# The low part of the attention scores: from two 64-row products to two 128-row products with zeros

## The chip, the cores and the metric

The kernel runs on one core of one Trainium2 chip. The metric is device time in microseconds (us), from the first to the last instruction of the program with what little lies around it; lower is better. The profile names the engines PE (TensorE, matrix products), PEld (the loads of its stationary operand), DVE (VectorE), ACT (ScalarE), POOL (GpSimd) and SP (which issues the transfers here).

## What is computed

A trunk of two layers over 1024 tokens of width 1024, in float32: differential attention with a gated MLP, then gated linear attention with a gated MLP, each behind an RMS norm. The change lies in the attention of the first layer. Cut to what matters:

```python
q_blocks = ...                                   # blocks of 128 query tokens
s = jnp.einsum('bqhmd,bkhmd->bhmqk', qb, k)      # 8 heads h, 2 maps m, 64 values d
p = jax.nn.softmax(jnp.where(mask, s, -jnp.inf), axis=-1)
a = p[:, :, 0] - lam * p[:, :, 1]
o = jnp.einsum('bhqk,bkhe->bqhe', a, v)
...
o = rms_norm(o, subln_gain) * (1.0 - lambda_init)
```

Each head has two maps of 64 values, each with a softmax of its own; the difference of the two weighs the values, and the head's output is normed over its 128 values.

## The kernel before, in words

**Precision.** PE multiplies operands of the type fp32r, which hold fewer bits than float32. So the kernel splits a float32 operand into a high part (a cast) and a low part (the rest), and adds three products: high by high, high by low, low by high. In the helper `mm3` these are lines L142 to L144.

**The scores.** For the scores two products take the place of three. For each map m a tile `QH[m]` of 128 rows holds the high part of the queries twice, in rows 0 to 63 and again in 64 to 127; `KS[m]` holds the high part of the keys beside their low part in the same manner (map 1 with the halves exchanged). One product over 128 rows (L766) therefore gives high by high and high by low. The third, low queries by high keys, is the second score product (L771). The low parts of both maps lie in one tile `QL`: map 0 in rows 0 to 63, map 1 in rows 64 to 127. So L771 contracts over 64 rows alone, map 0 over the upper half of PE's array and map 1 over the lower half.

**The loop.** `attention` runs over 8 heads, and in each over 8 query tiles i of 128 tokens. For tile i, w = (i + 1) * 128 keys count. For w up to 512 both maps share one PSUM tile of 1024 columns; for more, each map has its own, cut into two pieces (256 and 384 columns for i = 4; 512 and 256, 384 or 512 for i = 5 to 7). There are two such PSUM tiles. Behind the scores comes a chain: DVE takes mask and maximum out of PSUM (L776), ACT exponentiates (L779), POOL scales the second map (L783), DVE subtracts (L785). One tile later `transposes` turns the result on PE (`pta`, L802), ACT and DVE split it (`ah` L805, `al` L806), and every second tile `values` multiplies it with the values into `oT`.

**What fills PE meanwhile.** Between the score tiles of head h stand the units of head h + 1: the products for its queries, keys and values (`psq`, `psv`, 24 products of 512 columns for each unit), a transpose of its values (`psw`, L707), the rotary step and the stacking into `QH` and `KS`, in which POOL makes `QL` (L685; DVE does for head 0). In head 7 the first units of the output projection (`pacc`, `res` L325) stand there. Behind the last head comes the rest of that projection, and behind it the first MLP.

**The head's norm.** After every fourth tile `finish` squares `oT` on ACT (L829), keeps a scaled copy `on` (L831) in the buffer place 27, and splits the squares on DVE into `hl` (L284, L285, place 26). Later `rstd_rows` adds them over the rows on PE (`ssp`, L293 and L294), takes the reciprocal root with ACT's logarithm and exponential and some steps of DVE (L295 to L300, all in place 13), multiplies with `on` (L837) and writes the result to memory.

**What sets the order.** Each engine runs its instructions in one fixed order. That order is worked out when the kernel is built, by a planner that runs the program against its own table of costs; the kernel's text only gives the order in which work is offered to it. The buffers ("places", `slot(i)`) hold 128 rows of 1024 values each, and a new tile in a place waits for the readers of the one before it.

## Time and profile before

| | |
|---|---|
| median of three runs | 2517.71 us (2516.28 to 2519.01) |
| profiled execution: its time, its span | 2519.34 us, 2517.6 us |
| PE busy in the span | 2450.1 us (97%) |
| DVE, POOL, ACT busy | 65%, 47%, 41% |
| attention of layer 0, first score product to last transposes | about 64 to 536 us |
| one head of the middle (1 to 6) | 59.90 us |

In the timeline each row is an instruction or a run of equal ones: when the first starts, how long the row lasts, its engine, line and operation, the tile written and the tiles read, the shape, the count, and in brackets the idle time of the engine before it with what ended it. `128*128` or `64*128` ahead of a shape is the rows by columns of the stationary operand. PE's products are pipelined: a product's own length is longer than its distance to the next one, so that what a product costs PE is read from the start of one row to the start of another, not from its length or from the busy share.

### The profile page before, as it was taken

What the parts mean: (1) busy time and instruction counts of PE and PEld (TensorE: products, weight loads), DVE (VectorE), ACT (ScalarE), POOL (GpSimd) and SP (SyncE); (2) the same over time, 40 slices, a digit from 0 to 9 for tenths busy, and PEclk for the clock granted to TensorE, in tenths of its full rate; (3) what the DMA queues carried; (4) which work ended last, traced back from release to release, by engine and by line L of the source; (5) the groups of instructions that cost most, each with busy time, mean ns of one, the idle gap of its engine ahead of it and who ended that gap; (6) DMA issues with size and microseconds to landing.
All of it is one profiled execution on the core that took longest, in us unless ns stands there. A gap on an engine that the chain in (4) does not pass through costs nothing. (4 is left out here: it accounts for less than half of the span.)

```text
span 2517.6 us, 30784 instructions
## 1 busy us (share of the span) xinstructions
PE 2450.1 (97%) x11752; PEld 1995.8 (79%) x11752; DVE 1625.7 (65%) x2210; ACT 1040.6 (41%) x1630; POOL 1189.4 (47%) x723
## 2 busy tenths in 40 slices
PE   7999999998999999999999999999899999999998
PEld 6777777776788888878888998987678888887887
DVE  5577777877666666654565486487676666655455
ACT  4454544544454554432124443442345445443211
POOL 4444444425655555554423344343465555545441
PEclk9999999999999999999999999999999999999999
DMA  5222222433222222343321111124322222244331
GB/s 188 56 67 59 59 59 59 126 122 126 75 76 84 76 85 83 137 157 109 101 87 60 34 43 59 35 92 156 112 76 76 84 77 88 79 147 148 107 101 67
DMA packets 66020, 228.60 MB, mean 91 GB/s; under 512 B 8145, under 2 KB 8785, under 8 KB 65873
## 3 DMA queue, kind: packets, MB, share of 16 engines
q1 hardware_dynamic: 65872, 226.64, 27.3%
q8 instruction: 92, 1.51, 0.3%
q14 instruction: 56, 0.45, 0.1%
HBM read 163.17 MB, written 50.86 MB: 85 GB/s over the span
## 5 line engine op out<-in xcount | busy, mean ns | idle before, releaser
L325 DVE TENSOR_TENSOR res<-pacc,res 128x512 f32<-128x512 f32 x368 | 252.9, 690 | 238.1 <-PE pacc L144 237.6
L497 POOL TENSOR_TENSOR uw<-st,uw 128x512 fp32r<-128x512 f32 x190 | 290.9, 1532 | 219.8 <-ACT uw L496 212.1
L123 POOL TENSOR_TENSOR wl<-st,wh 128x1024 fp32r<-128x1024 f32 x57 | 146.0, 2568 | 203.6 <-ACT wh L122 203.6
L144 PE MATMUL pacc<-wdh,gl 128*128 128x512 f32 x512 | 200.8, 392 | 0.0
L143 PE MATMUL pacc<-wdl,gh 128*128 128x512 f32 x512 | 200.5, 392 | 0.0
L142 PE MATMUL pacc<-wdh,gh 128*128 128x512 f32 x512 | 198.6, 392 | 1.8 <-DVE res L316 1.8
L576 DVE SCALAR_TENSOR_TENSOR b<-cu,cv,b 128x1023 f32<-128x1023 f32 x44 | 63.4, 1440 | 172.5 <-ACT b L575 172.2
L496 ACT CAST uw<-st 128x512 fp32r<-128x512 f32 x190 | 118.0, 622 | 123.8 <-PE ps_z L144 54.2
L142 PE MATMUL psq<-XH,wh 128*128 128x512 f32 x384 | 156.6, 408 | 0.1
L143 PE MATMUL psq<-XL,wh 128*128 128x512 f32 x384 | 154.1, 401 | 0.1
L144 PE MATMUL psq<-XH,wl 128*128 128x512 f32 x384 | 152.6, 399 | 0.0
L626 POOL TENSOR_TENSOR gl<-st,gh 128x1024 fp32r<-128x1024 f32 x32 | 77.8, 2430 | 151.3 <-ACT gh L625 108.4
L779 ACT ACTIVATE p<-p,nmax 128x256 f32<-128x256 f32 (+7 forms) x128 | 99.1, 777 | 85.4 <-DVE nmax L776 84.2
L497 POOL TENSOR_TENSOR wh<-st,wh 128x512 fp32r<-128x512 f32 x56 | 87.1, 1555 | 80.8 <-ACT wh L496 80.8
L625 ACT CAST gh<-st 128x1024 fp32r<-128x1024 f32 x32 | 33.6, 1050 | 202.7 <-PE pacc L143 144.1
L497 POOL TENSOR_TENSOR wl<-st,wl 128x512 fp32r<-128x512 f32 x56 | 85.3, 1524 | 63.0 <-ACT wl L496 63.0
L142 PEld LDWEIGHTS pacc<-wdh,gh 128*128 128x128 f32 x512 | 96.1, 188 | 23.4 <-DVE res L316 2.6
L143 PEld LDWEIGHTS pacc<-wdl,gh 128*128 128x128 f32 x512 | 96.1, 188 | 21.7
L144 PEld LDWEIGHTS pacc<-wdh,gl 128*128 128x128 f32 x512 | 96.1, 188 | 20.9
L776 DVE CUSTOM_DVE_ANT_0 p<-s_ps,mask 128x256 f32<-128x256 f32 (+7 forms) x128 | 91.4, 750 | 30.7 <-PE pta L802 22.4
L142 PE MATMUL pacc<-wh,gh 128*128 128x512 f32 x256 | 103.2, 409 | 4.0 <-DVE res L325 4.0
L143 PE MATMUL pacc<-wl,gh 128*128 128x512 f32 x256 | 102.8, 403 | 1.5 <-POOL wl L123 1.5
(363 smaller groups left out, 7358.9 us busy)
## 6 DMA issues: line engine op xcount, KB each, us to landing
st<-in_wup_dram SPq DMA_DIRECT2D x88, 512.0 KB, 3.5
g_scr<-a SPq DMA_DIRECT2D x44, 512.0 KB, 2.6
st<-in_wdn_dram SPq DMA_DIRECT2D x44, 512.0 KB, 3.6
st<-g_scr SPq DMA_DIRECT2D x44, 512.0 KB, 3.3
r_scr<-res SPq DMA_DIRECT2D x24, 512.0 KB, 4.7
res<-r_scr SPq DMA_DIRECT2D x24, 512.0 KB, 5.7
st<-in_wqk_dram SPq DMA_DIRECT2D x16, 512.0 KB, 3.5
st<-o_scr SPq DMA_DIRECT2D x13, 512.0 KB, 3.3
```

Source lines behind the costliest of these rows:

```text
L123: (eng_lo or nc.gpsimd).tensor_tensor(lo, st, f32(hi), op=ALU.subtract)
L142: nc.tensor.matmul(ps, lhsT=ah, rhs=bh, start=first, stop=False, **kw)
L143: nc.tensor.matmul(ps, lhsT=ah, rhs=bl, start=False, stop=False, **kw)
L144: nc.tensor.matmul(ps, lhsT=al, rhs=bh, start=False, stop=last, **kw)
L325: nc.vector.tensor_tensor(res[t][:, half(dh)], ps, res[t][:, half(dh)], op=ALU.add)
L496: nc.scalar.copy(w[:, half(0)], src)
L497: nc.gpsimd.tensor_tensor(w[:, half(1)], src, f32(w[:, half(0)]), op=ALU.subtract)
L576: nc.vector.scalar_tensor_tensor(u[:, 1:], c[:, :T - 1], cv[:, n, 1:2], u[:, 1:], op0=ALU.mult, op1=ALU.add)
L625: nc.scalar.copy(hi, st)
L626: nc.gpsimd.tensor_tensor(lo, st, f32(hi), op=ALU.subtract)
L776: nc.vector.tensor_tensor_reduce(out=pm[:, :w], in0=s_ps[:, :w], in1=st["mask"][:, T - w:], scale=-0.125, scalar=3.0e38, op0=ALU.add, op1= ...
L779: nc.scalar.activation(pm[:, :w], pm[:, :w], AF.Exp, bias=nmax, scale=-1.0, accum_out=sums[:, m:m + 1])
```

## The change

The second score product contracts over 128 rows as the first does. A new tile `Z` (place 27, which `on` had) has for each map and for two query tiles at a time 128 rows by 256 columns of stationary operand. It is zeroed once by eight instructions on DVE; `low(h, g)` then copies, on ACT, the low parts of map 0 into its rows 0 to 63 and those of map 1 into its rows 64 to 127, each map into its own part, so that the rows of the other map stay zero. One such call serves the query tiles 2g and 2g + 1; `Z` holds two groups, and the copies for a group are offered two query tiles ahead of it: 64 copies of 64x256 in all. The product with all 128 rows of `KS[m]` then adds the same as the one over 64 rows did. For each map its two products now stand behind each other.

Since place 27 is taken, the norm of the head makes do with fewer places: `on` moves into the free half of the squares' tile, and the reciprocal root `y` goes into the place of `hl` (26 or 19), which is free by then; it is taken there only after the sums are read. The norm of the second layer passes its old place and is as before.

```diff
-            QH, QL, KS, _, _ = st[h]
+            QH, _, KS, _, _ = st[h]
...
+            if i % 2 == 0 and (i + 2 < NT or h + 1 < HEADS):
+                low(h + (i + 2) // NT, (i + 2) % NT // 2)
...
             for m in range(2):
-                for c, n in parts:
-                    nc.tensor.matmul(s[m][:, c:c + n], lhsT=QH[m][:, qt], rhs=KS[m][:, c:c + n],
-                                     start=True, stop=False)
-            for c, n in parts:
-                for m in range(2):
-                    rows = slice(64 * m, 64 * m + 64)
-                    nc.tensor.matmul(s[m][:, c:c + n], lhsT=QL[rows, qt], rhs=KS[m][rows, c:c + n],
-                                     start=False, stop=True)
+                for first, q in ((True, QH[m][:, qt]), (False, Z[:, i // 2 % 2, m, i % 2 * P:i % 2 * P + P])):
+                    for c, n in parts:
+                        nc.tensor.matmul(s[m][:, c:c + n], lhsT=q, rhs=KS[m][:, c:c + n],
+                                         start=first, stop=not first)
```

```diff
+        Z = slot(27, "Z", F32R, [P, 2, 2, 2 * P])
+        for n in range(8):
+            nc.vector.tensor_scalar(Z[:, n // 4, n // 2 % 2, n % 2 * P:n % 2 * P + P], ones_f, 0.0, None, op0=ALU.mult)
+
+        def low(h, g):
+
+            for m in range(2):
+                rows = slice(64 * m, 64 * m + 64)
+                nc.scalar.copy(Z[rows, g % 2, m, :], st[h][1][rows, g * 2 * P:(g + 1) * 2 * P])
...
+        low(0, 0)
```

```diff
-    def rstd_rows(hl, y, tmp, n):
+    def rstd_rows(hl, place, tmp, n):
...
         nc.vector.tensor_scalar(tmp, ss, 1.0 / n, EPS, op0=ALU.mult, op1=ALU.add)
+        y = place()
         nc.scalar.activation(y, tmp, AF.Ln)
...
-            ia, ion, ihl = (17, 18, 19) if h == HEADS - 1 and hf else (13, 27, 26)
+            last = h == HEADS - 1 and hf
+            ia, ihl = (17, 19) if last else (13, 26)
...
-            on = slot(ion, "on")[:, :512]
+            on = a[:, 1, :]
...
-                y = a[:, 1, :]
-                rstd_rows(hl, y, a[:, 0, :], P)
+                y = rstd_rows(hl, lambda: slot(ihl, "y")[:, :512], a[:, 0, :], P)
```

The planner's order moves with it, at three places that matter here. The first is PE in head 4: the last transposes of head 3, and the scores of the query tiles i = 2 and i = 3 (`s_ps`; `ks_2162` and `qh_2160` are map 0, `ks_2163` and `qh_2161` map 1). Before:

```order
L802 MATMUL pta<-ident,p_2657 128x128 x4
L766 MATMUL s_ps<-ks_2162,qh_2160 128x384
L766 MATMUL s_ps<-ks_2163,qh_2161 128x384
L771 MATMUL s_ps<-ks_2162,ql 128x384
L771 MATMUL s_ps<-ks_2163,ql 128x384
L766 MATMUL s_ps<-ks_2162,qh_2160 128x512
L766 MATMUL s_ps<-ks_2163,qh_2161 128x512
```

And with the change (`ks_2197`, `qh_2195` and `ks_2198`, `qh_2196` are the same two maps):

```order
L813 MATMUL pta<-ident,p_2700 128x128 x4
L782 MATMUL s_ps<-ks_2197,qh_2195 128x384
L782 MATMUL s_ps<-ks_2197,Z 128x384
L782 MATMUL s_ps<-ks_2198,qh_2196 128x384
L782 MATMUL s_ps<-ks_2198,Z 128x384
L782 MATMUL s_ps<-ks_2197,qh_2195 128x512
L782 MATMUL s_ps<-ks_2197,Z 128x512
```

There are as many products as before, in the same stretches between the same transposes; within a stretch each map is now done with before the other begins.

The second place is ACT at the start of head 4, from the copy of the values (`vt`) to the exponentials of the query tile i = 2. Before:

```order
L701 COPY vt<-psv 128x512 [waits PE_49]
L805 CAST ah<-pta 128x4x128 [waits DVE_49,PE_49]
L805 CAST ah<-pta 128x3x128 [waits DVE_49,PE_49]
L779 ACTIVATE p_2733,sums<-p_2733,nmax 128x128 [waits DVE_49]
L805 CAST ah<-pta 128x4x128 [waits PE_49]
L779 ACTIVATE p_2733,sums<-p_2733,nmax 128x128 [waits DVE_49]
L779 ACTIVATE p_2809,sums<-p_2809,nmax 128x256 [waits DVE_49] x2
L805 CAST ah<-pta 128x4x128 [waits PE_49]
L779 ACTIVATE p_2878,sums<-p_2878,nmax 128x384 [waits DVE_49] x2
```

And with the change:

```order
L703 COPY vt<-psv 128x512 [waits PE_49]
L759 COPY Z<-ql 64x256 [waits PE_49] x2
L816 CAST ah<-pta 128x4x128 [waits DVE_49,PE_49]
L816 CAST ah<-pta 128x3x128 [waits DVE_49,PE_49]
L790 ACTIVATE p_2776,sums<-p_2776,nmax 128x128 [waits DVE_49]
L816 CAST ah<-pta 128x4x128 [waits PE_49]
L790 ACTIVATE p_2776,sums<-p_2776,nmax 128x128 [waits DVE_49]
L790 ACTIVATE p_2853,sums<-p_2853,nmax 128x256 [waits DVE_49] x2
L759 COPY Z<-ql 64x256 [waits PE_49]
L759 COPY Z<-ql 64x256 [waits PE_49,Activation_49]
L816 CAST ah<-pta 128x4x128 [waits PE_49]
L790 ACTIVATE p_2923,sums<-p_2923,nmax 128x384 [waits DVE_49] x2
```

Four of a head's eight copies stand there, two ahead of the first casts and two ahead of the last one; each waits until PE has read the group that lay in `Z` before. Of the other four, two stand ahead of the exponentials of i = 5 and two by the casts ahead of those of i = 7.

The third place is PE at the start of the first MLP, far behind the attention: the transposes of the last token block (`pt<-ident,hn`, four each) and the MLP's product with the sum S2 (`ps_x<-S`). Before:

```order
L232 MATMUL pt_5763<-ident,hn 128x128 x4
L232 MATMUL pt_5778<-ident,tmp 128x128 x4
L232 MATMUL pt_5793<-ident,hn 128x128 x4
L142 MATMUL ps_x<-S_5235,uw_5711 128x512
...
L144 MATMUL ps_x<-S_5236,uw_5711 128x512
L232 MATMUL pt_5778<-ident,hn 128x128 x4
```

And with the change:

```order
L232 MATMUL pt_5851<-ident,tmp 128x128 x4
L232 MATMUL pt_5836<-ident,hn 128x128 x4
L232 MATMUL pt_5851<-ident,hn 128x128 x4
L232 MATMUL pt_5866<-ident,hn 128x128 x4
L142 MATMUL ps_x<-S_5308,uw_5784 128x512
```

Four transposes that stood behind the twelve products now stand ahead of them.

More of the change, by code (lines that the diff above doesn't have):

```diff
@@ L300, in rstd_rows @@
         nc.vector.scalar_tensor_tensor(y, tmp, 1.5, y, op0=ALU.add, op1=ALU.mult)
+        return y
     def accumulate_tiles(res, ts, pairs):
@@ L1127, in normed @@
         def normed(hd, hf, a, hl):
-            y = a[:, 1, :]
-            rstd_rows(hl, y, a[:, 0, :], DV)
+            y = rstd_rows(hl, lambda: a[:, 1, :], a[:, 0, :], DV)
             for e in range(2):
```

## The prediction

> **What bounds the kernel now.** I read the page's busy shares first, then the stretches of single heads, then who waits for whom in the attention, and last the timeline of PE around the score products.
>
> ```profile
> PE 2450.1 (97%) x11752; PEld 1995.8 (79%) x11752; DVE 1625.7 (65%) x2210; ACT 1040.6 (41%) x1630; POOL 1189.4 (47%) x723
> ...
> 300.30:360.20 59.90, 58.79 (x301) 45.80 (x300) 45.18 (x90) 29.83 (x62) 29.94 (x20) 1.00 0.22 62
> 480.00:536.00 56.00, 51.88 (x277) 39.66 (x277) 48.47 (x95) 28.96 (x60) 14.22 (x11) 1.00 0.25 78
> ```
>
> In the second row, head 4, the columns behind the length are busy PE, PEld, DVE, ACT and POOL and the granted clock. PE is busy for 58.79 of 59.90 us, DVE for 45.18, ACT for 29.83, and heads 1 to 6 repeat this. So PE sets the pace, and what a score product costs PE comes back as time. In the last row, head 7, DVE works for 48.47 of 56 us, and less of a gain on PE can be kept.
>
> ```profile
> PE ssp L293 <- DVE hl L284: 3.1, 7, 0.5
> PE oT L142 <- ACT ah L805: 2.4, 9, 0.5
> ```
>
> These are PE's longest summed waits of this stage beside one transfer: about 0.5 us for `ssp` in each head, and a few tenths for `oT`. Where such a wait stands right behind a score block, a shorter block only lengthens the wait.
>
> **The pitch of PE.** Products over 128 rows that follow each other, by first and last row:
>
> ```profile
> 312.37 0.45 PE L142 MATMUL psq<-XH,wh 128*128 128x512 f32 x1
> 318.03 0.39 PE L293 MATMUL ssp<-hl,ones 128*128 128x512 f32 x1
> ...
> 301.79 0.28 PE L144 MATMUL oT<-ah,vl 128*128 128x256 f32 x1
> 303.35 0.22 PE L142 MATMUL oT<-ah,vh 128*128 128x128 f32 x1
> 303.63 1.39 PE L802 MATMUL pta<-ident,p 128*128 128x128 f32 x11
> ```
>
> 24 products of 512 columns take 318.03 - 312.37 = 5.66 us, 0.236 each. 13 of 256 columns take 1.56 us, 0.12 each. 11 of 128 columns last 1.39 us, up to 0.126 each; I take 0.12. For 384 columns I take three quarters of 0.236, 0.177.
>
> **What a change of tiles costs now.** The scores of i = 2 and 3 of head 4, and behind them two products of 256 columns:
>
> ```profile
> 305.18 0.61 PE L766 MATMUL s_ps<-ks,qh 128*128 128x384 f32 x2 [0.17 <-DVE nmax L776]
> 306.10 0.73 PE L766 MATMUL s_ps<-ks,qh 128*128 128x512 f32 x2
> 306.75 0.50 PE L771 MATMUL s_ps<-ks,ql 64*128 64x512 f32 x2
> 307.19 0.39 PE L142 MATMUL oT<-ah,vh 128*128 128x256 f32 x1
> 307.41 0.60 PE L802 MATMUL pta<-ident,p 128*128 128x128 f32 x4
> ...
> 350.74 0.63 PE L766 MATMUL s_ps<-ks,qh 128*128 128x512 f32 x2
> 352.61 0.49 PE L771 MATMUL s_ps<-ks,ql 64*128 64x512 f32 x1
> 353.03 0.87 PE L802 MATMUL pta<-ident,p 128*128 128x128 f32 x6
> ```
>
> One 64-row product lasts 0.49 us (352.61), two of them together 0.50 (306.75): the halves of the array work side by side, and the pair saves one pitch of 0.236. Yet from 306.10 to 307.41 four products of 512 columns and one of 256 take 1.31 us; less 0.12 that is 1.19, where four pitches are 0.94 and three, with the pair side by side, 0.71. So going over to 64 rows and back costs 1.19 - 0.71 = 0.48 us and gains 0.24. [...]
>
> **The change on PE, block by block.** As many products stay; each gets the pitch of 128 rows.
>
> - i = 2 and 3: from 305.18 to 307.41 are 2.23 us; 4 x 0.177 + 4 x 0.236 + 0.12 = 1.77. Of the 0.46 I take 0.40, as the first product behind a wait starts slowly either way.
>
> ```profile
> 300.30 0.34 PE L766 MATMUL s_ps<-ks,qh 128*128 128x128 f32 x2
> ...
> 310.15 0.46 PE L766 MATMUL s_ps<-ks,qh 128*128 128x256 f32 x2
> 311.25 0.28 PE L144 MATMUL oT<-ah,vl 128*128 128x256 f32 x1
> ...
> 324.33 0.54 PE L766 MATMUL s_ps<-ks,qh 128*128 128x256 f32 x2
> 325.54 0.39 PE L142 MATMUL oT<-ah,vh 128*128 128x256 f32 x1 [0.18 <-ACT ah L805]
> ...
> 332.62 0.94 PE L766 MATMUL s_ps<-ks,qh 128*128 128x512 f32 x4
> 334.05 0.50 PE L142 MATMUL psq<-XH,wh 128*128 128x512 f32 x1
> ...
> 341.14 0.98 PE L766 MATMUL s_ps<-ks,qh 128*128 128x512 f32 x4
> 343.19 0.50 PE L293 MATMUL ssp<-hl,ones 128*128 128x512 f32 x1 [0.46 <-DVE hl L284]
> ```
>
> - i = 0 and 1: 300.30 to 301.79, 1.49 us, less 4 x 0.12 + 4 x 0.12 + 0.12 = 1.08: 0.41.
> - i = 4, map 0: 310.15 to 311.25, 1.10, less 2 x 0.12 + 2 x 0.177 + 0.12 = 0.71: 0.39.
> - i = 4, map 1: 324.33 to 325.54 is 1.21, without the wait 1.03, and would be 0.59. But `oT` waits for ACT's cast, which no score product releases: nothing, at most 0.44.
> - i = 5: 1.43 against 4 x 0.236 + 4 x 0.12 = 1.42: nothing, since here all 64-row products come in pairs and pay the change once.
> - i = 6: 2.05 less the wait of 0.46 is 1.59, against 4 x 0.236 + 4 x 0.177 = 1.65; 0.06 longer, out of the wait for `ssp`.
> - i = 7: 350.74 to 353.03 are seven products in 2.29, less 7 x 0.236 = 1.65: 0.64. The eighth stands ahead of an `oT` that waits for a cast: nothing.
>
> Sum 0.40 + 0.41 + 0.39 + 0.64 = 1.84 us a head, 11.0 for heads 1 to 6. From below it is 1.03 (i = 4 and 7 alone, if the waits on DVE around i = 0 to 3 take their gain); from above 1.84 + 0.44 + 0.1.
>
> Head 0 starts at half clock in part, head 7 waits for DVE:
>
> ```profile
> 63.67 0.53 PE L766 MATMUL s_ps<-ks,qh 128*128 128x128 f32 x2 [2.37 <-DMA ks<-kl]
> 71.11 0.47 PE L802 MATMUL pta<-ident,p 128*128 128x128 f32 x1
> 64.00:70.00 6.00, 6.00 (x21) 3.59 (x21) 3.94 (x17) 3.85 (x13) 0.81 (x3) 0.58 0.29 90
> ...
> 507.50 0.52 PE L766 MATMUL s_ps<-ks,qh 128*128 128x512 f32 x2
> 509.58 0.66 PE L802 MATMUL pta<-ident,p 128*128 128x128 f32 x4
> ```
>
> In head 0 from 63.67 to 71.11 stand the scores of i = 0 to 3, half of those of i = 4 and four transposes: 12 x 0.12 + 4 x 0.177 + 4 x 0.236 + 2 x 0.297 = 3.69 us at full clock, 6.4 at the clock of 0.58, against 7.44: 1.1. Its later blocks, which hold fewer pairs, add about 1.0 by the middle heads. Together 2.1, between 0.8 and 3.5. In head 7 the two halves of i = 4 take 2.08 us, which would be 4 x 0.12 + 4 x 0.177 = 1.19: 0.89; with 0.81 for i = 0 to 3 that makes 1.7, and I count nothing behind it, where DVE is behind. Between 0.8 and 4.
>
> **The copies on ACT** hide in ACT's waits:
>
> ```profile
> L805 ACT CAST ah<-pta 128x512 fp32r<-128x512 f32 x45 | 26.4, 586 | 53.2 <-PE pta L802 53.2
> L805 ACT CAST ah<-pta 128x256 fp32r<-128x256 f32 x16 | 6.0, 373 | 6.5 <-PE pta L802 6.5
> 304.29 0.97 ACT L805 CAST ah<-pta 128x512 fp32r<-128x512 f32 x2 [2.49 <-PE pta L802]
> 308.05 0.59 ACT L805 CAST ah<-pta 128x512 fp32r<-128x512 f32 x1 [0.55 <-PE pta L802]
> 338.49 0.94 ACT L779 ACTIVATE p<-p,nmax 128x768 f32<-128x768 f32 x1 [5.00 <-DVE nmax L776]
> ```
>
> No row has a 64x256 copy; a cast of as many columns lasts 0.373 us, so two last 0.75, eight 3.0 a head, on an ACT that has some 30 us idle there. Two stand ahead of the casts at 304.29, behind 2.49 us of idle time; two ahead of the cast at 308.05, with 0.55; two ahead of 338.49, with 5.00. Queued behind them are casts that `oT` needs and exponentials. Only at 308.05 is something late, by 0.2 us, and its reader on PE comes 2 us later. I take 0.1 a head, 0.7 in all; without the cover one pair would cost 0.75 a head, 6 us. The eight zeroings on DVE fall into the first microseconds, in which DVE waits for the input; with the casts of the norm, as many as before, they cost nothing.
>
> **The first MLP's start.**
>
> ```profile
> 642.08 1.09 PE L232 MATMUL pt<-ident,hn 128*128 128x128 f32 x4 [1.34 <-DVE S L238]
> 642.82 0.78 PE L142 MATMUL ps_x<-S,uw 128*128 128x512 f32 x1
> ```
>
> PE waits for DVE here, and four transposes take 0.74 us. Four more now stand ahead of the product, and the last four wait for a further result of DVE. Taken later they would have cost PE less: I take a loss of 0.7, between 0 and 3.
>
> **The sum**: -11.0 - 2.1 - 1.7 + 0.7 + 0.7 = -13.4 us. The profiled execution took 2519.34 us (span 2517.6), so 2505.9; the median of the runs shown, 2517.71, lies 1.6 lower: 2504 us.
>
> **The rivals.**
>
> *The waits take most of it.* The chain from scores over DVE, ACT and POOL to `pta` paces a head as soon as PE is faster; the waits on `hl` and `ah` speak for it, DVE's 14.7 us of idle time in head 4 against it. Then only half of the 1.03 of each head stays, 3.1 for six, 1.6 for the two others, less 1.4: -3.3, 2514 us.
>
> *More of it.* The first map's scores are done earlier, as they no longer stand behind the other map's, so DVE starts earlier and the waits shrink as well: 2.4 x 6 + 3.5 + 4 = 21.9 less 0.7, 2496 us. For it speaks that DVE's mask step reads map 0 first; against it that most of these waits hang on other work.
>
> *The pairs were worth it.* The side-by-side halves are lost, and what I read as the cost of changing tiles is a late start that 128-row products have in these places too. Then each pair costs one pitch more: for i = 0 to 3, 5 and 6 that is 128 + 256 + 384 + 512 + 768 + 896 = 2944 columns, 1.36 us a head, 10.9 in all, 2529 us. It decides where the excess of a block stays above 0.24. The seven products of i = 7, most of them unpaired, speak against it: they lose 0.64 with nothing saved, and the single transposes behind 128-row products keep their pitch.
>
> That the change does not do what it says is ruled out by the order: all 192 products read `Z`.
>
> **How the numbers follow.** I give the forecast 0.70, the waits 0.12, more 0.13, the pairs 0.05. With the bounds above the forecast itself spans 2498 to 2510. To leave out no more than 2 in 10, the range reaches over most of both rivals on the faster side: 2495 to 2513. A measurement tells 0.2%, 5 us, from no change, so faster means below 2512.7: 0.70 + 0.13 + 0.04 of the waits = 0.87; the same 0.08; slower 0.05.
>
> **What would show it.** Right: a middle head of about 58 us for 59.90; rows of `Z` that follow each other by 0.236 for 512 columns; from 128-row score products to `oT` no gap; copies of 0.4 us in ACT's idle time. Wrong: score blocks as long as before; waits of PE on `ah`, `nmax` or `p` that grow by as much as the blocks shrink; a wait for a copy on ACT; a start of the MLP later by more than the attention is earlier.

## The result and the profile after

The changed kernel took 2502.45 us (median of four runs, 2501.07 to 2502.74) against 2517.01 for the kernel before on the same chip: a ratio of 0.9945, 95% interval 0.9934 to 0.9957. The prediction was 2504. The profiled execution took 2502.59 us with a span of 2500.6, 17.0 less than the span before; the profiled execution before lay 2.3 us above its median, so that the medians differ by 14.6 and the profiled times by 16.8.

In the changed kernel both score products stand at L782, the copies into `Z` at L759, `pta` at L813, the cast `ah` at L816 and the subtraction `p` at L796. First the line of busy shares, then its stretches of head 0, head 1, head 4, head 6 and of head 7 to the last `oT`. The columns behind the length are busy PE, PEld, DVE, ACT and POOL, the granted clock and the DMA share.

```profile
PE 2428.0 (97%) x11752; PEld 2005.6 (80%) x11752; DVE 1628.8 (65%) x2218; ACT 1064.3 (43%) x1694; POOL 1196.0 (48%) x723
...
64.36:115.49 51.13, 50.16 (x238) 41.25 (x239) 33.31 (x74) 25.55 (x57) 27.89 (x20) 0.97 0.24 63
115.49:174.93 59.44, 56.72 (x301) 47.16 (x300) 48.12 (x92) 33.64 (x72) 29.66 (x20) 1.00 0.23 63
290.84:348.80 57.96, 56.66 (x301) 47.18 (x300) 45.27 (x90) 32.95 (x70) 29.70 (x20) 1.00 0.23 64
406.77:470.52 63.75, 60.84 (x325) 50.97 (x324) 48.57 (x93) 35.37 (x73) 32.18 (x21) 0.97 0.40 120
470.52:531.33 60.81, 56.55 (x311) 47.70 (x310) 48.44 (x95) 32.79 (x67) 14.29 (x11) 0.97 0.26 84
```

The same for head 0 and head 6 of the kernel before:

```profile
63.67:121.10 57.43, 56.59 (x239) 41.66 (x239) 33.97 (x78) 23.98 (x51) 26.80 (x20) 0.91 0.22 58
420.13:482.98 62.85, 61.73 (x325) 48.37 (x324) 48.07 (x92) 32.33 (x65) 30.83 (x21) 1.00 0.38 111
```

PE still sets the pace. Head 4 is 1.95 us shorter and its ACT has 3.1 us more to do. (The 59.90 us given for one head of the middle hold for heads 2 to 5 alone: before the change head 1 took 59.38, and head 6 took 62.85 with 325 products on PE for 301.) But the heads are not equally shorter: head 0 lost 6.3 us, with a granted clock of 0.97 for 0.91; head 1 lost nothing; head 6 is longer, and its clock is below 1.00 now. The starts of the first score product of each head give this account of the 16.9 us between the two last products (2510.23 and 2493.30 us):

| stretch | before, us | after, us | difference |
|---|---|---|---|
| start to head 0 | 63.67 | 64.36 | +0.69 |
| head 0 | 57.42 | 51.14 | -6.28 |
| head 1 | 59.38 | 59.44 | +0.06 |
| heads 2 to 5, together | 239.65 | 231.84 | -7.81 |
| head 6 | 62.85 | 63.75 | +0.90 |
| head 7 to the last `oT` | 64.13 | 60.81 | -3.32 |
| from there to the first product of the MLP | 80.88 | 80.85 | -0.03 |
| the rest | 1882.24 | 1881.11 | -1.13 |

The timeline of PE after the change, score tiles i = 0, 2 and 3 of head 4:

```profile
290.84 0.22 PE L782 MATMUL s_ps<-ks,qh 128*128 128x128 f32 x1
290.90 0.28 PE L782 MATMUL s_ps<-ks,Z 128*128 128x128 f32 x1
291.01 0.27 PE L782 MATMUL s_ps<-ks,qh 128*128 128x128 f32 x1
291.12 0.27 PE L782 MATMUL s_ps<-ks,Z 128*128 128x128 f32 x1
...
295.28 0.44 PE L782 MATMUL s_ps<-ks,qh 128*128 128x384 f32 x1 [0.17 <-DVE nmax L787]
295.56 0.33 PE L782 MATMUL s_ps<-ks,Z 128*128 128x384 f32 x1
...
296.08 0.40 PE L782 MATMUL s_ps<-ks,qh 128*128 128x512 f32 x1
296.32 0.40 PE L782 MATMUL s_ps<-ks,Z 128*128 128x512 f32 x1
296.55 0.39 PE L782 MATMUL s_ps<-ks,qh 128*128 128x512 f32 x1
296.78 0.39 PE L782 MATMUL s_ps<-ks,Z 128*128 128x512 f32 x1
```

Products of 512 columns now follow each other by 0.23 to 0.24 us, those of 128 by 0.11, whichever operand they read. Summed over head 4, the distance from a product to the next one, waits included, fell by 1.28 us on the score products, by 0.38 on the products of `oT` with 256 columns, 0.22 on the transposes and 0.06 on `psq`. So a third of the price of the change of tiles stood in the rows behind the score products.

PE's waits in the attention, summed (us in total, times, longest):

```profile
PE oT L142 <- ACT ah L816: 6.8, 16, 1.8
PE pta L813 <- DVE p L796: 4.0, 2, 2.4
PE s_ps L782 <- DMA ks<-kl: 2.4, 1, 2.4
PE ssp L293 <- DVE hl L284: 1.8, 7, 0.3
```

The wait for `hl` fell from 3.1 to 1.8, the one for `ah` grew from 2.4 to 6.8. In head 4 the first gives 0.2 us back and the second takes 0.4. The 2.4 us in the row of `pta` stand at the end of head 7, where 2.5 stood before the change. The two new long waits are single ones, 1.59 in head 1 and 1.83 in head 6. In head 1 (POOL, DVE, PE; then DVE before the change):

```profile
117.30 2.38 POOL L123 TENSOR_TENSOR wl<-st,wh 128x1024 fp32r<-128x1024 f32 x1 [7.36 <-ACT wh L122]
117.36 3.40 DVE L796 SCALAR_TENSOR_TENSOR p<-p,rc,p 128x1024 f32<-128x1024 f32 x1
120.91 0.52 PE L813 MATMUL pta<-ident,p 128*128 128x128 f32 x3 [1.59 <-DVE p L796]
```

```profile
121.03 1.28 DVE L785 SCALAR_TENSOR_TENSOR p<-p,rc,p 128x1024 f32<-128x1024 f32 x1
```

The subtraction of 1.28 us lasts 3.40 where it begins just behind an operation of POOL of 2.38 us, and PE waits 1.59 us for it. POOL ends at 119.68 and DVE 1.08 us later, at 120.76, though it began 2.3 us before POOL's end. The other heads show the same: over both kernels this subtraction of 1024 columns took 3.08 to 3.40 us in the four places where POOL's `wl` had begun first, one of them at the end of head 6 before the change, and 1.28 or 1.29 in the eleven where it began before `wl`.

In head 6 (POOL, ACT, ACT, PE):

```profile
455.54 3.33 POOL L695 TENSOR_TENSOR kl<-kr,ks 128x1024 fp32r<-128x1024 f32 x1
458.91 1.05 ACT L128 CAST gh<-st 128x1024 fp32r<-128x1024 f32 x1 [1.38 <-POOL kl L695]
459.86 0.85 ACT L816 CAST ah<-pta 128x512 fp32r<-128x512 f32 x2
460.49 0.38 PE L142 MATMUL oT<-ah,vh 128*128 128x256 f32 x1 [1.83 <-ACT ah L816]
```

The cast `gh` for the output projection waits for POOL and stands ahead of the cast that PE needs. ACT had the same order before, with 1.21 us of the same wait, and PE came later:

```profile
472.56 1.05 ACT L128 CAST gh<-st 128x1024 fp32r<-128x1024 f32 x1 [1.21 <-POOL kl L693]
```

After the change the clock falls to half at 462.05 us, 1.6 us behind the end of PE's wait, for 3.41 us, of which half, 1.7 us, is lost.

### The profile page after: what moved, and what is told of

Read it like the earlier page. It is cut to its first block, busy times and chain, and to the rows that moved or that the text cites. A ratio compares the mean times of both kernels' runs of the same rounds, so it can differ in the third digit from the quotient of the medians.

```text
span 2500.6 us, 30864 instructions
## 1 busy us (share of the span) xinstructions
PE 2428.0 (97%) x11752; PEld 2005.6 (80%) x11752; DVE 1628.8 (65%) x2218; ACT 1064.3 (43%) x1694; POOL 1196.0 (48%) x723
## 5 line engine op out<-in xcount | busy, mean ns | idle before, releaser
L122 ACT CAST wh<-st 128x1024 fp32r<-128x1024 f32 x59 | 61.5, 1047 | 97.0 <-PE psq L143 49.9
```

The lines of the kernel that those rows point to most:

```text
L122: nc.scalar.copy(hi, st)
```

## The experiments

All times of heads are from the first score product of one to that of the next; head 7 reaches to its last `oT`. They come from one profiled execution of each kernel, the medians from 4 to 11 runs. "Half clock" is the stretch at half the TensorE clock that begins within 3 us of head 0's start. The kernel before had medians of 2517.25 to 2518.30 in the four groups of runs.

| kernel | median, us | head 0 | head 1 | 2 to 5, mean | head 6 | head 7 | half clock, us |
|---|---|---|---|---|---|---|---|
| before | 2517.01 | 57.42 | 59.38 | 59.91 | 62.85 | 64.13 | 10.24 |
| the change | 2502.45 | 51.14 | 59.44 | 57.96 | 63.75 | 60.81 | 3.41 |
| norm's places alone | 2517.95 | 57.28 | 59.37 | 59.92 | 62.82 | 65.26 | 10.24 |
| 128 rows, old order | 2503.79 | 51.88 | 59.44 | 57.98 | 62.83 | 59.51 | 3.41 |
| 64 rows, map by map | 2539.03 | 60.93 | 61.66 | 62.99 | 65.48 | 63.92 | 13.65 |
| pairs kept at i = 5, 6 | 2504.99 | 54.70 | 57.63 | 57.95 | 62.26 | 61.98 | 3.41 |
| pairs in head 0, i < 4 | 2505.11 | 54.83 | 59.49 | 57.96 | 62.38 | 60.58 | 10.24 |
| no copies | 2499.33 | 51.69 | 57.62 | 57.99 | 62.24 | 60.27 | 3.41 |
| copies on POOL | 2506.32 | 54.97 | 57.48 | 57.58 | 62.86 | 66.51 | 3.41 |
| `gh` later | 2502.59 | 51.10 | 59.46 | 57.97 | 64.27 | 59.89 | 3.41 |
| `res` behind the keys | 2504.15 | 51.12 | 59.35 | 57.93 | 58.62 | 62.70 | 3.41 |
| both | 2501.70 | 51.23 | 59.43 | 57.94 | 57.93 | 65.99 | 3.41 |

### Which part of the change makes the gain

**The norm's places alone.**

```diff
-            on = slot(ion, "on")[:, :512]
+            on = a[:, 1, :]
...
-                y = a[:, 1, :]
-                rstd_rows(hl, y, a[:, 0, :], P)
+                y = rstd_rows(hl, lambda: slot(ihl, "y")[:, :512], a[:, 0, :], P)
```

> The kernel before with the norm's fewer places alone: the scaled copy in the free half of the squares' tile, the reciprocal root in the place of the split squares; the score products as they were. My theory: nothing, 2517, 2513 to 2520, middle heads of 59.9 us. Rival, the places let PE go on earlier at the ends of the heads: 2503 to 2512. Second rival, the place of hl is held longer, so that the next split waits: slower, up to 2525.

Measured: 2517.95, ratio 0.9999 (0.9990 to 1.0008). The places are worth nothing, and both rivals fall.

**The 128 rows alone, in the old order.**

```diff
+            for m in range(2):
+                for c, n in parts:
+                    nc.tensor.matmul(s[m][:, c:c + n], lhsT=QH[m][:, qt], rhs=KS[m][:, c:c + n], ...)
             for c, n in parts:
                 for m in range(2):
-                    nc.tensor.matmul(s[m][:, c:c + n], lhsT=QL[rows, qt], rhs=KS[m][rows, c:c + n], ...)
+                    nc.tensor.matmul(s[m][:, c:c + n], lhsT=Z[:, ..., m, ...], rhs=KS[m][:, c:c + n], ...)
```

> The changed kernel with the old order of the products: first the first products of both maps, then the 128-row products from Z, piece by piece and map by map within it. Only the rows are changed against the kernel before. My theory, the rows alone make the gain: a middle head of 57.9 to 58.2 us, in all 2502, 2498 to 2507. Rival, the order of the maps is worth something (the first map is ready earlier): 2507 to 2517, the longer heads by longer waits of the next product on DVE.

Measured: 2503.79, ratio 0.9943 (0.9930 to 0.9955), the same as the whole change; heads 2 to 5 take 57.98. The rows make the gain, and the order of the maps adds nothing that can be seen.

**The order alone, with 64 rows.**

```diff
             for m in range(2):
+                rows = slice(64 * m, 64 * m + 64)
                 for c, n in parts:
                     nc.tensor.matmul(..., lhsT=QH[m][:, qt], ...)
-            for c, n in parts:
-                for m in range(2):
-                    rows = slice(64 * m, 64 * m + 64)
+                for c, n in parts:
                     nc.tensor.matmul(..., lhsT=QL[rows, qt], rhs=KS[m][rows, c:c + n], ...)
```

> The kernel before with one part of the change alone: the two products of a map stand behind each other, map by map, but the second keeps its 64 rows. So no 64-row products of the two maps are neighbours any more, and each map of each query tile goes to 64 rows and back. My theory: 0.48 for each map of i = 0 to 3 (3.84 us a head in place of 0.81), 0.96 for i = 5, 6 and 7 each, nothing new for i = 4, which stood map by map already: about 5 us a head slower, 40 us in all, some of it in the waits: 2550 us, 2535 to 2560. Rival, the order of the maps is what pays, since DVE gets its first map earlier: below 2517, down to 2503. Second rival, changes of tiles are free and only the pairs count: 1.36 us a head, 2528.

Measured: 2539.03, ratio 1.0086 (1.0072 to 1.0099): slower, in my range, though 11 us below its middle. Both rivals fall; the second one's 2528 is too little, since heads 3 and 5, at full clock, are already 2.3 us longer and heads 2 and 4 hold a stretch of half clock besides. Of the 5 us a head that I expected, the score products of head 3 show 3.5; the products behind them take 0.6 less and the waits 0.6 less, which leaves the 2.3. My sum was too high in one place that the trace of before shows: i = 7 stood map by map already (two full products and two of 64 rows in one half from 350.74 us on), so its 0.96 was no loss.

### What a change of tiles costs by itself

**Twelve streams of products** with an idle stretch ahead of each.

```diff
+    def pairs(n):
+        stream(n, lambda j: (full if j in (0, 1, 94, 95) else halfrow, j % 2))
+    def two_and_pair(n):
+        stream(n, lambda j: (full if j % 4 < 2 else halfrow, j % 2))
+    def six_and_pair(n):
+        stream(n, lambda j: (full if j % 8 < 6 else halfrow, j % 2))
```

> None of the model is computed here (the output is zeros): one tile of random stationary values, one moving tile, and twelve streams of 96 products each, every product with another part of the stationary tile, with an idle stretch of DVE work ahead of each stream. Streams of 512 columns: all over 128 rows; pairs of 64 rows (upper and lower half of the array in turn); 64 rows of one half alone; two of 128 rows and a pair in turn; six of 128 rows and a pair; 128, 128, 64 and 128 rows in turn. Then full rows, pairs, two and a pair with 256 and with 128 columns. My theory (going to 64 rows and back costs 0.48 us, a pair takes the time of one product): 0.236 a product over 128 rows; 0.118 in the stream of pairs; (3 x 0.236 + 0.48) / 4 = 0.297 for two and a pair; (7 x 0.236 + 0.48) / 8 = 0.267 for six and a pair; (4 x 0.236 + 0.48) / 4 = 0.356 for the single one; with 256 columns 0.21 for two and a pair against 0.12, with 128 columns about 0.17. Rival, the excess in the kernel is a late start and the change is free: 0.177 for two and a pair, 0.207 for six and a pair, 0.236 for the single one. Second rival, 64-row products never lie side by side: 0.236 in the stream of pairs, and then a change costs half of what I said. For the half clock at the start of a stream I have no number; what I want to see is whether streams of 64 rows stay at half clock longer than those of 128 rows, as head 0 of the kernel before did (10.2 us against 3.4).

The stretches of six streams: pairs, 64 rows of one half, two and a pair, six and a pair (all with 512 columns), two and a pair with 256, full rows with 128:

```profile
53.49:66.92 13.43, 13.43 (x96) 10.29 (x96) 0.00 (x0) 0.00 (x0) 0.00 (x0) 0.86 0.00 0
81.06:122.36 41.30, 41.30 (x96) 31.00 (x96) 0.00 (x0) 0.00 (x0) 0.00 (x0) 0.50 0.00 1
136.74:180.99 44.25, 44.25 (x96) 18.57 (x96) 0.00 (x0) 0.00 (x0) 0.00 (x0) 0.50 0.00 0
195.54:221.55 26.01, 26.01 (x96) 16.10 (x96) 0.00 (x0) 0.00 (x0) 0.00 (x0) 0.90 0.00 1
341.02:370.13 29.11, 29.11 (x96) 18.59 (x96) 0.00 (x0) 0.00 (x0) 0.00 (x0) 0.50 0.00 1
383.93:404.26 20.33, 20.33 (x96) 20.33 (x96) 0.00 (x0) 0.00 (x0) 0.00 (x0) 0.50 0.00 0
```

At full clock a product over 128 rows takes 0.227 us, a pair of 64 rows 0.227 as well (0.113 each), and eight products with one pair among them 1.99 to 2.02, where seven pitches are 1.59: going over and back costs 0.40 to 0.43, not 0.48, and neither rival's number appears. The last column but two is what I had not expected: four of these streams never came to full clock, though PE is busy in every microsecond of them.

**Blocks in a stream at full clock**, so that only the price is seen.

```diff
+    BLOCKS = ([],
+              [(F, 0, 512), (F, 1, 512), (U, 0, 512), (U, 1, 512)], [(F, 0, 512), (F, 0, 512), (F, 1, 512), (F, 1, 512)],
...
+        for n in range(16):
+            for form, m, c in [(F, i % 2, 512) for i in range(8)] + block:
```

> None of the model is computed here (the output is zeros): one unbroken stream of products on PE, in which a block of score-like products stands 16 times behind eight 128-row products of 512 columns each, so that the clock stays full. Blocks: two full products and a pair of 64 rows against four full ones, with 512, 384, 256 and 128 columns; two full ones and two of 64 rows in one half; two, one of 64 rows and one; two and two pairs; one, one of 64, one, one of 64. From the first streams: going to 64 rows and back cost 1.993 - 7 x 0.227 = 0.404 us at full clock (six and a pair) and 0.406 (one single product in four), not the 0.48 that I read in the kernel. My theory, the price does not hang on the columns: a block with a pair takes 0.404 less one pitch more than the four full ones, 0.17 with 512, 0.23 with 384, 0.28 with 256, 0.30 with 128; two of 64 rows in one half 0.40 more; two pairs 0.404 - 2 x 0.227 = 0.05 less than six full products; two separate singles 0.81 more. Rival, the price grows with the columns (it is the last product's own run through the array): 0.17 with 512, but 0.05 or less with 128. Second rival, two pairs in a row pay twice: 0.35 more.

Sixteen repetitions of eight full products and a block: a pair and four full ones with 512, then with 256, then with 128 columns; last two pairs:

```profile
41.26:87.90 46.64, 46.64 (x193) 31.66 (x192) 0.00 (x0) 0.00 (x0) 0.00 (x0) 1.00 0.00 0
87.90:131.55 43.65, 43.65 (x194) 36.15 (x193) 0.00 (x0) 0.00 (x0) 0.00 (x0) 1.00 0.00 1
...
216.69:257.92 41.23, 41.23 (x194) 31.64 (x193) 0.00 (x0) 0.00 (x0) 0.00 (x0) 1.00 0.00 0
257.92:295.02 37.10, 37.10 (x195) 31.75 (x193) 0.00 (x0) 0.00 (x0) 0.00 (x0) 1.00 0.00 1
295.02:334.64 39.62, 39.62 (x195) 31.65 (x193) 0.00 (x0) 0.00 (x0) 0.00 (x0) 1.00 0.00 0
334.64:371.08 36.44, 36.44 (x194) 31.22 (x193) 0.00 (x0) 0.00 (x0) 0.00 (x0) 1.00 0.00 1
...
471.42:521.94 50.52, 50.52 (x225) 33.44 (x223) 0.00 (x0) 0.00 (x0) 0.00 (x0) 1.00 0.00 1
```

Per block the pair is longer than four full products by (46.64 - 43.65) / 16 = 0.19 us with 512 columns, 0.19 with 384, 0.26 with 256 and 0.20 with 128. Two of 64 rows in one half cost 0.41 more than full rows, one single 0.40, two separate singles 0.82; two pairs in a row 50.52 against 43.65 + 32 x 0.227 = 50.91, 0.02 less a block. Going over and back costs that loss and the pitch that the pair saved: about 0.41 us with 512 columns, 0.36 with 384, 0.38 with 256 and 0.31 with 128. So the price falls by a quarter where the columns fall to a quarter; I had no fall at all (a loss of 0.30 for 128), and both rivals are far off. Two pairs in a row pay it once.

**Pairs kept where they come in twos**, at i = 5 and 6: there stand the lines of the kernel before, elsewhere those of the change.

```diff
+            if i in (5, 6):
...
+            else:
```

> The changed kernel, but the query tiles i = 5 and 6 keep the 64-row pairs and the old order, two pairs in a row for each tile. My theory: two pairs pay one change of 0.404 and save 0.236 + 0.12 (i = 5) and 0.236 + 0.177 (i = 6): 0.05 longer and 0.01 shorter a head, nothing in all: 2500 to 2504.5, the heads 2 to 5 at 57.9 to 58.1 us. Rival, pairs are worth their pitches: 0.77 a head, 6 in all, 2496. Second rival, each change costs 0.40 and nothing is saved: 0.8 a head, 2509.

Measured: 2504.99, ratio 0.9949 (0.9935 to 0.9962). Heads 2 to 5 take 57.95 for 57.96: in the kernel two pairs in a row cost and save nothing, as I said. "Pairs are worth their pitches" falls. The total is 0.5 above my range: head 0 is 3.6 longer, 2.1 of it a wait of `ssp` on `hl`, and head 1 gives 1.8 back, since there DVE's subtraction begins ahead of POOL's `wl` and takes its 1.28 us.

### The clock at the start of head 0

PE at the start of head 0: before, then after in three stretches.

```profile
64.93:75.17 10.24, 10.24 (x28) 6.69 (x29) 6.18 (x24) 5.54 (x18) 2.14 (x4) 0.50 0.16 51
```

```profile
64.36:66.10 1.74, 1.74 (x14) 1.74 (x15) 1.02 (x7) 0.69 (x2) 0.44 (x1) 1.00 0.40 49
66.10:69.51 3.41, 3.41 (x12) 2.90 (x11) 3.00 (x11) 3.36 (x13) 0.45 (x1) 0.50 0.35 136
69.51:75.17 5.66, 5.66 (x27) 4.57 (x26) 3.42 (x10) 2.79 (x10) 1.99 (x3) 1.00 0.00 0
```

Half clock for 10.24 us against 3.41: of the 6.83 us between them half, 3.4 us, is lost. Is it the rows, or luck? In the next kernel the pairs, in the old order, stay in four tiles of head 0 alone.

```diff
+            if h == 0 and i < 4:
...
+            else:
```

> The changed kernel, but in head 0 alone the query tiles i = 0 to 3 keep the 64-row pairs in the old order. My theory, from the first streams (two full products and a pair in turn never came to full clock, full ones after one or two stretches of 3.41 us): the clock at the start of head 0 stays at half for 10.24 us in place of 3.41, which costs 3.4 us, and the tiles' own price is 0.9: head 0 at about 55.4 us for 51.1, in all 2506.5, 2504.5 to 2508. Rival, the half clock is luck of the moment: 3.41 us of it, head 0 at 52 us, 2503.3.

Its head 0 and the stretch at half clock:

```profile
63.90:118.72 54.82, 53.85 (x238) 42.54 (x239) 33.17 (x74) 24.28 (x53) 28.07 (x20) 0.91 0.22 58
64.12:74.36 10.24, 10.24 (x32) 7.05 (x32) 5.92 (x25) 5.62 (x18) 2.02 (x4) 0.50 0.17 53
```

The 10.24 us are back, head 0 is 3.7 longer than with the change, and the median is 2505.11, ratio 0.9944 (0.9931 to 0.9958), in my range. The medians alone would not tell this kernel from the change; the trace does. One of the five runs took 2501.08, at a mean granted clock of 0.995 for 0.991 or 0.992 in the others, so the length of the stretch is likely not the same in every execution. Over all kernels of the table, each one with 64-row products in the first tiles of head 0 has 10.24 or 13.65 us, and each one without has 3.41.

The traces say more. All changes of the clock in a trace lie on one grid of 3.413 us. For each window of that grid the share of the array in use can be estimated from the starts of the products: 0.427 us at half clock for one of 512 columns and 128 rows (their distance in the first stream), in proportion less for fewer columns or rows. At the start of head 0 the windows at half clock behind which the clock stayed at half hold 0.41 to 0.65, all of them in the four kernels with 64-row products there; those behind which it opened hold 0.75 or more, in all twelve. So the 64-row tiles keep the clock down in these traces (10.24 us and more for 3.41), and a PE that is busy throughout does not open it by that alone (41.30 us at half clock in the stream of 64 rows of one half). That the share of the array is what counts is an inference from this, which the streams bear out in the main. By the rows and columns used, 64 rows of one half are 0.5 of the array, two and a pair 3 x 0.427 us in 1.87, 0.68; both stayed at half clock to their end. Six and a pair, 7 x 0.427 in 3.58, 0.83, opened after 5.2 us. Pairs with 256 columns, 0.213 us each at half clock and so the whole array, opened after 4.35 us; pairs with 128 columns take the same 0.213 us, 0.5 of the array, and stayed at half for all of their 10.8 us. The bound is not sharp, or not this alone: with one single in four (0.65) the clock opened after 26 us. The stretches of 3.41, 10.24 and 13.65 us are one, three and four steps of the grid; what sets the grid, no trace shows.

### The copies

**Without them.**

```diff
-                nc.scalar.copy(Z[rows, g % 2, m, :], st[h][1][rows, g * 2 * P:(g + 1) * 2 * P])
+                if h == 0 and g == 0:
+                    nc.scalar.copy(Z[rows, g % 2, m, :], st[h][1][rows, g * 2 * P:(g + 1) * 2 * P])
```

> The changed kernel without the copies of the low parts on ACT, but for the first four (so the third part of the scores, low queries by high keys, is taken from wrong or zero values; that part of the computation is left out). The products are all there. My theory: the copies cost what the waits of PE on ACT's casts grew by, up to 0.3 us a head, and the 1.83 us of head 6 with the half clock behind it (1.7): 2497 to 2501. Rival, they are hidden and head 6's wait is the cast that waits for POOL, with or without copies: 2501 to 2503. Second rival, they cost their own length on the path (24 us of ACT's time, 3.0 a head): 2478.

The copies themselves, in the changed kernel:

```profile
L759 ACT CAST Z<-ql 64x256 fp32r<-64x256 f32 x64 | 25.8, 403 | 15.0 <-POOL ql L687 10.0 <-PE s_ps L782 4.1
```

Measured: 2499.33, ratio 0.9928 (0.9915 to 0.9940), in my range; the interval overlaps that of the change. The number came out, its reason did not. The heads 2 to 5 are as long without 3.2 us of copies each as with them: there the copies are hidden wholly. What is gained lies in heads 1 and 6, by 1.8 and 1.5 us. In head 1 DVE begins ahead of POOL. In head 6 the wait of PE on ACT is still there, 1.9 us, and the cast `gh` ahead of `ah` waits 2.15 us for POOL; so it is that cast, as the first rival has it, and not the copies. What is missing is the stretch of half clock behind the wait.

**On POOL.**

```diff
-                nc.scalar.copy(Z[rows, ...], ...)
+                nc.gpsimd.tensor_copy(Z[rows, ...], ...)
```

> The changed kernel with the copies of the low parts on POOL in place of ACT. The run without them left the heads 2 to 5 as long as they were, so ACT's copies cost nothing there. My theory: PE bounds these heads with some 15 us of idle time on the engines behind it, so the copies are hidden on POOL as well: heads 2 to 5 at 57.9 to 58.1 us, 2500 to 2504. Rival: POOL and DVE keep each other out (a subtraction of DVE took 3.40 us for 1.28 beside one of POOL's), and POOL stands in the chain from the scores to pta, so copies there delay p: PE waits for p or nmax, 0.3 to 1 us a head, 2505 to 2511.

Measured: 2506.32, ratio 0.9959 (0.9946 to 0.9972). A miss on both sides: the total lies in the rival's range, but the middle heads got shorter, 57.58, against what the rival says, and the whole got longer than I said. The loss is at the ends: in head 0 `ssp` waits 2.6 us for `hl` and a second stretch of half clock comes, head 7 begins with a wait of 3.9 us for its keys:

```profile
PE ssp L293 <- DVE hl L284: 2.6, 1, 2.6
...
PE s_ps L782 <- DMA ks<-kl: 3.9, 1, 3.9
```

### The end of head 6

**The cast `gh` later.**

```diff
+                with tc.issue_after(held[0].ins) if held and self.base == 0 else nullcontext():
                     self.prepare((0, 1))
```

(`held` is the last cast `ah` offered by then.)

> The changed kernel with one cast moved on ACT: the first cast of the output projection (gh, L128), which stood ahead of the cast ah in head 6 and waited for POOL, is held back behind the casts of that query tile, so that oT does not wait for it. My theory: PE's wait of 1.83 us on ah in head 6 shrinks to 0.2, and the half clock of 3.41 us that begins 1.6 us behind it goes away with it (1.7 us): 2499, 2497.5 to 2500.5, head 6 at about 60.3 us for 63.75. Rival, the wait only moves: the projection's first products (pacc) wait for gl instead, or the next wait on POOL takes its place: 2501 to 2503. Rival for the clock: the half clock is not caused by the wait and stays: 2500.5.

PE at the start of head 7 in this kernel, and the transfer that it waits for (KB each, median us from issue to landing):

```profile
471.27 0.30 PE L783 MATMUL s_ps<-ks,qh 128*128 128x128 f32 x1 [3.40 <-DMA ks<-kl]
...
ks<-kl SPq DMA_DIRECT2D x2, 256.0 KB, 11.0
```

Measured: 2502.59, ratio 0.9940 (0.9927 to 0.9952). The wait on `ah` went, and my theory fell all the same: the rival was right that the wait only moves, though it moved to a transfer, which the rival did not name. Head 7's keys land late, and the half clock moved with the wait (472.40 us).

**The residual behind the keys.** The two transfers of the keys run among six loads of `res`, 512 KB each, on one queue, whose packets fill 75.2% of the time of the 16 DMA engines from 450 to 475 us, and they take 8.8 us in head 6 of the changed kernel (8.6 before the change). One head earlier, from 390 to 415 us, it is 28.9%, and they take 3.4:

```profile
ks<-kl SPq DMA_DIRECT2D x2, 256.0 KB, 8.8
...
ks<-kl SPq DMA_DIRECT2D x2, 256.0 KB, 3.4
```

```diff
-                with tc.issue_after(last_load[-1].ins):
+                with tc.issue_after((keys if self.base == 0 else last_load)[-1].ins):
                     for t in early:
                         load(t)
```

> The changed kernel with the loads of the residual held back behind the transfers of head 7's keys, and the cast gh where it was, ahead of ah. My theory: head 6 still has its wait of 1.83 us on ah, with the half clock behind it, as the cast gh waits for POOL and not for a transfer; the keys no longer bound the start of head 7, but nothing is gained as PE comes there later anyway: 2501 to 2503. Rival, the transfers were what made head 6 long in the changed kernel too: 2497 to 2499.5.

> The changed kernel with two things moved at the end of head 6: the cast gh held back behind the casts of that query tile, as in the kernel before this one, and the loads of the residual (res, 512 KB each), which stand ahead of the two transfers of head 7's low keys (ks<-kl) on SP's queue, held back behind them. In the kernel with gh alone held back PE waited 3.40 us for ks<-kl, which took 11.0 us to land where it takes 3.4 in head 6's predecessors. My theory: the transfers share the DMA engines with the loads; without them ahead the keys land some 5 us earlier and the wait goes, with it the half clock of 3.41 us behind it (1.7 us): 2502.6 - 3.4 - 1.7 = 2497.5, 2495.5 to 2499, head 6 at 59.5 to 61 us. Rival, the keys are late for another reason (POOL makes kl late): the wait stays above 2 us, 2501 to 2503. Second rival, the residual now comes too late for the first sums of the projection: a wait of pacc on it, 2500 to 2504.

Measured: 2504.15 (ratio 0.9942, 0.9930 to 0.9954) with the loads alone held back, 2501.70 (0.9936, 0.9923 to 0.9948) with `gh` too. The keys then land in 3.1 and 3.6 us, and no wait on them is left, as the theory says. But both theories miss: 2504.15 is above my range for the loads alone, where the wait on `ah` did not stay but shrank from 1.83 to 0.89 us, and 2501.70 is above the 2499 that I allowed with `gh` too; the rivals' ranges hold that number, but neither rival's wait is in the trace. Neither kernel can be told from the change. With the loads alone PE comes to the first product of the MLP at 608.84 us for 612.19, about the 3.4 us that the stretches of half clock at 462.05 and 520.08 had cost, which are gone; behind it 3.3 us are lost again, 1.7 of them in more half clock and 1.6 in a wait of the MLP's products on ACT (`rv`, 6.5 us for 4.9). With both, head 6 takes 57.93 for 63.75, and head 7 5.2 more: it now holds 24 of the `oT` products and transposes that stood in head 6, and one stretch of half clock is left. None of these versions beats the change by more than a measurement tells.

## Why the prediction was right, and where it was not

The time was right, 2502.45 for 2504, and the cause was: going over to 64-row tiles and back costs PE 0.40 to 0.43 us in the streams, and full rows, 0.227 us each there, pay nothing of it. What PE does in these 0.4 us no run shows. Of the terms:

- **Heads 2 to 5**: -1.84 each predicted, -1.95 measured. The price of a change was read as 0.48 and is 0.40 to 0.43 in a stream; a single pair of 512 columns loses 0.19 where I had 0.24. The two separate singles of i = 7 were 0.64 and i = 5 and 6 nothing, and the runs agree with both.
- **Head 1**: -1.84 predicted, +0.06 measured. The step "only at 308.05 is something late" looked at ACT alone. POOL's `wl` came 4.9 us earlier than before and DVE's subtraction 3.7, so that the two met with POOL first; 1.59 us of wait took the gain. In the kernel without copies and the one with pairs at i = 5 and 6 DVE is first, and head 1 takes 57.62 and 57.63 us, which is nearly the predicted gain. It is the first rival at one place.
- **Head 6**: -1.84 predicted, +0.90 measured: a wait on POOL, hidden before, came to PE (1.83), and a stretch of half clock behind it (1.7). With `gh` out of the way the landing of the keys was the next wait. I had taken head 6 as a middle head without looking at what it holds for the projection.
- **Head 0**: -2.1 predicted (0.8 to 3.5), -6.28 measured, outside its bounds. The mis-sized step is "6.4 at the clock of 0.58": I took the clock as given. It was part of what the change changes, and 3.4 of the 6.3 are its shorter stretch. The other 2.9 lie in the bounds.
- **Head 7**: -1.7 predicted (0.8 to 4), -3.32 measured, in its bounds; I counted nothing behind i = 4, and those tiles kept their gain too.
- **The copies**: +0.7 predicted, nothing in heads 2 to 5. The estimate of 0.373 us for one was near (0.403).
- **The start of the MLP**: +0.7 predicted, nothing measured: 80.85 for 80.88 us from the last `oT`.
- Not foreseen: +0.69 ahead of head 0, and -1.13 behind the start of the MLP, where one stretch of half clock (1836 us before, 1821 after) is 3.41 shorter.

So two errors, head 0 too small by 4.2 and heads 1 and 6 too large by 4.6, cancelled each other; the right total is partly luck. Of the rivals, "waits take most of it" was true of two heads in eight. "More of it" falls too: its 3.5 for head 0 is 2.8 short, and its cause, the order of the maps, is worth nothing, as the old order with 128 rows is as fast. "The pairs were worth it" is refuted by the pairs at i = 5 and 6 and by the blocks.

## What to carry to other kernels

A product over half of the rows was not a cheap product among full ones here: with 512 columns a single one cost 0.40 us more than a full one, and a pair 0.19 more than two full ones, so that filling the other half with zeros was faster, where an idle engine could fill the tile; two pairs in a row broke even (0.02 us less). When the busiest engine gets faster, look at the first and last rounds of a loop before you multiply the gain of a middle one: there the next wait stands close behind, and here heads 1 and 6 fell 4.6 us short of their part, a third of the 13.4 expected, by two single waits and the half clock behind one of them. Where the trace shows a slower clock, ask what the change does to the clock before using it as a factor.

## What the runs showed of the hardware

- PE's clock stayed at half through 41.30 us of back-to-back 64-row products in one half of the array, 44.25 us of two full products and a pair in turn, and 20.33 us of full 128x128 products, with PE busy all the time. Full rows with 512 columns came to full clock after 4.0 us, by the starts of their products (19 in the first 6.2 us, where 0.227 us each makes 27).
- Half clock comes in stretches of 3.41 us or multiples, except for the last of a trace. A wait of PE of 1.83 us at the end of head 6 was followed by one (1.6 us behind its end) in the changed kernel, and by none in the kernel with pairs at i = 5 and 6, and the one of 1.85 us without copies was followed by none either. One of 3.40 us, with `gh` later, was (1.1 us behind). In three kernels in which the wait there was 0.9 us none stood behind it. The grid of 3.413 us explains most of this: by the same estimate as for head 0, the window with the wait holds 0.39 of the array in the changed kernel and 0.42 in the one with pairs, and without copies the wait is split between two windows of 0.52 and 0.66. At the end of head 7 all twelve kernels have a wait of 2.4 to 2.5 us: eight with a window of 0.24 or less went to half, the four whose emptiest window held 0.28 to 0.37 did not. So where a wait falls in the grid counts beside its length; elsewhere both outcomes occur between 0.2 and 0.4, so that no sharp bound is shown. From the MLP's start to the last product, a part whose text is the same in all of these kernels, the time varied from 1879.3 to 1884.4 us, in part with such stretches: differences of some 3 us between two such kernels say little.
- Products with 128 columns follow each other by 0.11 us at full clock in the changed kernel, half of the 0.227 that those with 512 take in the streams and not a quarter; with 256 it is 0.12.
- Where this subtraction on DVE and POOL's `wl` met, whoever came second waited: DVE 3.40 us for 1.28 in the changed kernel; without the copies, where DVE began first, POOL took 3.10 for 2.38 and no wait reached PE.
